# A depthwise convolution inside a tuned kernel: from diagonal products and VectorE taps to 128x32 products over shifted copies

## The chip, the cores and the metric

The kernel runs on one core of a Trainium2 chip. It is one program of 256 tokens through a stack of layers. The metric is the device time in microseconds; below, PE is TensorE (matrix products and transposes), DVE is VectorE, ACT is ScalarE, and SP is the engine whose queue issues nearly all DMAs.

## The reference, cut to what matters

The network is six feed-forward blocks with four mixers between them, each behind a norm; activations are 256 x 1024 in float32. The change is in the first mixer, which joins a convolution module and a sliding-window attention:

```python
z = h @ w_in                        # u, gate (512 each), q (512), k, v (128 each)
a = u * sigmoid(gate)               # 256 tokens x 512 channels
y = conv_general_dilated(a, w, padding=[(30, 0)],   # 31 taps, causal,
        feature_group_count=512) + b                # each channel by itself
yf = layer_norm(y) * ln_g + ln_b    # over the 512 channels
a_out = silu(yf)
b_out = sliding_window_attention(q, k, v, sinks)
return concatenate([a_out, b_out]) @ w_out
```

So output channel c at token t is a sum of 31 products of one channel's own past: `y[t, c] = sum_j w[j, c] * a[t - 30 + j, c] + b[c]`. The other parts in their order: two feed-forward blocks around this mixer and one behind it (F1, then the mixer "even", F3, F4), forgetting attention (fox), a feed-forward block (F6), an mLSTM mixer, a feed-forward block (F8), an attention with relative positions (rel), a last feed-forward block (F10) and a norm.

## The kernel before, in words

**Tiling.** The 256 tokens are two blocks b = 0 and 1 of 128 tokens. A projection is written as three products in a reduced float32 format (`mm3`): operands are split into a high and a low part (`hl` for weights, `xt` for activations), and high*high, high*low and low*high are added in PSUM. Each has 128 rows of the sum, 128 tokens as weight columns and 512 (at times 256) moving columns. Weights come from DRAM in units of 1024 columns into tiles of tag `b4`, and VectorE and ScalarE split them (`split`). Products of attention, and of the convolution, are in plain float32 and are recorded by the profiler twice each; transposes (`tr`) are products with an identity.

**Who sets the order.** The program is recorded first (`Rec`), each operation with an engine, an estimated duration, a key and the tiles it reads and writes; a line number in the trace is therefore that of a helper (`mm` L280, its matmul call at L293; `tr` L295, L298; `load` L300, L302; `store` L314, L316; `act` L199, L213; `tt` L220, L223; `stt` L237, L242). Then `schedule` (L319) simulates the engines: on each, among the operations that are ready at its time, the lowest key goes first, and a tile gets a buffer of its tag when one comes free. What results is a fixed order for each engine, written out as such. A table `NUDGE` shifts the keys of single labels by a number of weight units; `TAGS` sets columns and counts of the buffers (tag, type, columns, buffers, place), `CFG` a few leads. The two PSUM tags `acc` and `mm` have four banks of 512 columns each.

**The stage of the convolution** (`even`, L1260). Both blocks' u and gate are projected; ScalarE takes tanh of the gate, VectorE multiplies, and PE transposes the 128 x 512 result (L1298 to 1301) so that channels lie on partitions: four channel tiles of 128. ScalarE copies them behind 30 columns of zeros into two `aT` tiles, which hold 286 columns for each channel tile. Then with `cg=6` six quarters (8 taps each, 7 in the last) of the 31 taps are done on PE: channel tile 0 wholly, and the last two quarters of channel tile 1. Each tap is a product of a 128x128 diagonal matrix of its weights with the tap's 128 shifted columns, for each block by itself. The diagonals are loaded from DRAM, 8 taps in one tile. The other 75 of the multiply-adds (half of tile 1, all of tiles 2 and 3) run on VectorE over both blocks at once, 256 columns each:

```python
r.mm(bank[:, 0:P], d[:, j * P:(j + 1) * P], tap(ct, b * P + 8 * q + j, P), ...)   # PE
r.stt(ys, tap(ct, j, 2 * P), w, ys, ALU.mult, ALU.add)                            # VectorE
```

Results lie in the tile y (`yT`). For each block PE transposes y back, VectorE takes mean and variance (L1400), ScalarE normalizes, PE transposes again, and the activation follows; then the output projection (`outproj`) runs over four operand tiles, first those of the attention (2, 3), then those of the convolution (0, 1). Queries, keys, scores and softmax of the attention lie between.

**The start.** `consts` (L502) loads the input x in four pieces of 128x512, two for each block, with keys -30 + 0.15 b + 0.75 h, so the first halves of both blocks come before the second halves.

## Time and profile before

| | us |
|---|---|
| three runs | 1587.45, 1584.86, 1586.29 |
| median | 1586.29 |
| profiled execution, its own time | 1587.08 |
| its span in the trace | 1585.3 |
| PE busy | 1548.6 |
| DVE busy | 1217.4 |
| ACT busy | 938.1 |

Busy time counts an engine's instructions where at least one is running. The span goes from the first to the last instruction; the profiled execution takes 1.8 us longer than it. PEclk is the share of TensorE's full clock that was granted. A duration of one PE record is longer than the distance to the next, since products are pipelined: rates are read from blocks of many, durations from the last of a block. "Idle before" and the releaser in brackets tell what an engine waited for.

### The profile page before, as it was taken

The page shows a single profiled execution, that of the slowest core. Times are in us where ns is not written, and L with a number is a line of the kernel's source. Part 1 is how long each engine was busy: PE and PEld are TensorE (multiplying, and loading weights), DVE is VectorE, ACT ScalarE, POOL GpSimd, SP SyncE. Part 2 cuts the span into 40 slices and gives each one's busy share as a digit, 9 for nine tenths or more (in the row PEclk, how much of TensorE's full clock was granted, in tenths as well). Part 3 has the DMA queues.
Part 4 walks back from the last instruction along what each step waited for, and adds up shares of the span by engine and source line. Part 5 has one row for each costly group of instructions (what it writes and reads, how often), then busy time and mean ns, then how long its engine had stood idle before and what let it go on. Part 6 is the DMA issues. An engine that isn't in the chain of part 4 may idle for free.

```text
span 1585.3 us, 21242 instructions
## 1 busy us (share of the span) xinstructions
PE 1548.6 (98%) x7546; PEld 1266.6 (80%) x7546; DVE 1217.4 (77%) x2137; ACT 938.1 (59%) x1480; POOL 1.9 (0%) x8
## 2 busy tenths in 40 slices
PE   8999999999999999999999999999999999999998
PEld 6888878788887888787787887788877887788886
DVE  6555689798878869776899687898788674788784
ACT  6444545865555656456875565656566566765562
POOL 0000000000000000000000000000000000000000
PEclk9999999999999999999999999999999999999999
DMA  8556466447474475643664475455463755464560
GB/s 329 199 186 210 164 219 222 136 169 232 146 269 156 152 242 166 223 155 125 208 207 166 168 259 196 130 184 188 158 212 134 245 174 178 165 216 149 188 231 35
DMA packets 86779, 296.92 MB, mean 187 GB/s; under 512 B 9552, under 2 KB 13072, under 8 KB 86672
## 3 DMA queue, kind: packets, MB, share of 16 engines
q1 hardware_dynamic: 86384, 295.03, 55.1%
q8 instruction: 59, 0.97, 0.2%
q10 hardware_dynamic: 288, 0.52, 0.1%
q14 instruction: 48, 0.39, 0.1%
HBM read 294.44 MB, written 1.08 MB: 186 GB/s over the span
## 4 chain that ended last, share of the span: by engine, by line
PE 90%; DVE 6%; ACT 1%; issue 1%; DMA 1%; SPq 0%; POOLq 0%; POOL 0%; DVEq 0%; ACTq 0%
PE mm L293 59%; PE acc L293 27%; PE mm L298 4%; DVE hl L223 1%; DVE b L242 1%; DVE s L242 1%; ACT b L213 1%; DVE b L223 1%; DMA b<-in_w 1%; DVE x L242 1%; DMA x<-in_x 0%; DVE xt L223 0%; DVE s L233 0%; DVE b L254 0%; ACT L213 0%
## 5 line engine op out<-in xcount | busy, mean ns | idle before, releaser
L293 PE MATMUL mm<-hl,xt 128*128 128x512 f32 (+1 forms) x4104 | 983.6, 393 | 5.6 <-DVE xt L223 1.9
L293 PEld LDWEIGHTS mm<-hl,xt 128*128 128x128 f32 x4104 | 758.1, 188 | 168.7 <-DVE xt L223 4.8
L223 DVE TENSOR_TENSOR hl<-b,hl 128x1024 fp32r<-128x1024 f32 (+1 forms) x554 | 660.7, 1212 | 147.5 <-PE mm L293 70.5
L213 ACT ACTIVATE hl<-b 128x1024 fp32r<-128x1024 f32 (+1 forms) x554 | 572.5, 1052 | 325.4 <-PE mm L293 196.3
L293 PE MATMUL acc<-hl,gt 128*128 128x512 f32 x1584 | 385.7, 393 | 1.2 <-DVE gt L223 0.7
L293 PEld LDWEIGHTS acc<-hl,gt 128*128 128x128 f32 x1584 | 296.8, 189 | 63.9 <-DVE gt L223 1.9
L213 ACT ACTIVATE b<-mm,s 128x256 f32<-128x256 f32 (+2 forms) x150 | 77.3, 520 | 157.6 <-PE mm L293 151.1
L223 DVE TENSOR_TENSOR b<-b,b 128x1024 f32<-128x1024 f32 (+2 forms) x112 | 116.8, 1057 | 10.9 <-DMA b<-in_w 10.1
L298 PE MATMUL mm<-cst,b 128*128 128x128 f32 (+1 forms) x648 | 96.2, 276 | 9.7 <-DVE b L223 4.3
L298 PEld LDWEIGHTS mm<-cst,b 128*128 128x128 f32 (+1 forms) x648 | 77.5, 141 | 32.7 <-DVE b L223 7.0
L242 DVE SCALAR_TENSOR_TENSOR b<-mm,s,b 128x256 f32<-128x256 f32 x102 | 48.9, 479 | 63.2 <-ACT b L213 62.9
L293 PE MATMUL acc<-hl,xt 128*128 128x512 f32 x384 | 93.2, 395 | 0.9 <-DVE hl L223 0.9
L213 ACT ACTIVATE b<-b,s 128x256 f32<-128x256 f32 (+2 forms) x184 | 77.8, 450 | 24.9 <-DVE b L223 14.9
L293 PEld LDWEIGHTS acc<-hl,xt 128*128 128x128 f32 x384 | 70.6, 188 | 17.3 <-DVE hl L223 1.3
L223 DVE TENSOR_TENSOR gt<-mm,gt 128x512 fp32r<-128x512 f32 (+1 forms) x72 | 46.1, 642 | 32.7 <-ACT gt L213 32.4
L213 ACT ACTIVATE gt<-mm 128x512 fp32r<-128x512 f32 (+1 forms) x72 | 39.7, 553 | 41.7 <-PE mm L298 37.8
L213 ACT ACTIVATE b<-mm 128x512 f32<-128x512 f32 (+3 forms) x84 | 45.2, 546 | 13.8 <-PE mm L298 10.7
L242 DVE SCALAR_TENSOR_TENSOR s<-s 128x1 f32<-128x1 f32 (+2 forms) x248 | 45.4, 183 | 7.4
L213 ACT ACTIVATE b<-x 128x512 f32<-128x512 f32 x44 | 27.5, 627 | 25.8 <-DVE x L223 12.4
L242 DVE SCALAR_TENSOR_TENSOR hl<-b,cst,hl 128x512 fp32r<-128x512 f32 x48 | 33.1, 745 | 7.7 <-issue 7.6
L213 ACT ACTIVATE hl<-b,cst 128x512 fp32r<-128x512 f32 x48 | 32.7, 719 | 4.1 <-PE mm L293 3.3
L213 ACT ACTIVATE xt<-mm 128x512 fp32r<-128x512 f32 x40 | 23.4, 593 | 15.8 <-PE mm L298 14.9
(79 smaller groups left out, 597.9 us busy)
## 6 DMA issues: line engine op xcount, KB each, us to landing
b<-in_w SPq DMA_DIRECT2D x512, 512.0 KB, 5.1
g<-in_gains SPq DMA_DIRECT2D x16, 512.0 KB, 6.8
b<-in_diag SPq DMA_DIRECT2D x8, 512.0 KB, 4.6
b<-dr SPq DMA_DIRECT2D x16, 256.0 KB, 5.7
g<-in_relb SPq DMA_DIRECT2D x4, 512.0 KB, 4.7
b<-in_diag SPq DMA_DIRECT2D x4, 448.0 KB, 7.9
x<-in_x SPq DMA_DIRECT2D x4, 256.0 KB, 2.8
b<-in_w SPq DMA_DIRECT2D x4, 256.0 KB, 6.0
```

What stands on the lines that cost most here:

```text
L213: return self.nc.scalar.activation(self.res(out), self.res(in_), func, **kw)
L223: lambda: self.nc.vector.tensor_tensor(self.res(out), self.res(a), self.res(b), op), key=key)
L242: lambda: self.nc.vector.scalar_tensor_tensor(self.res(out), self.res(a), self.res(s), self.res(b), op0, op1, **kw), key=key)
L293: lambda: self.nc.tensor.matmul(self.res(out), self.res(l), self.res(r), start=start, stop=stop, **(dict(skip_group_check=True) if again e ...
L298: lambda: self.nc.tensor.transpose(self.res(out), self.res(in_), self.res(ident)), key=key)
```

## The change

The convolution goes wholly to PE, and VectorE does none of it.

- The transposed a goes into one tile `aT` of tag `b4`, 128 partitions x 4 channel tiles x 288 columns (30 of zeros, 256 tokens, 2 of zeros), with one ScalarE copy for each block. SP stores it to a new DRAM tile `da` of 512 rows (channels) x 288 columns, in two pieces: 158 columns for block 0, 130 for block 1.
- For each channel tile SP loads the weights (`cw`, 128 x 1024) and, for q = 0 to 3, the rows of `da` shifted by q columns: 32 partitions x 4 groups x 284 columns. Partition 32 q + c of the tile `taps` then holds channel c of each group g of 32 channels, shifted by q.
- A product with 128 rows (4 shifts x 32 channels) and 32 weight columns therefore sums four taps of 32 channels: 8 steps m of 4 taps make the 31 (the 32nd has weight zero), and four groups g write to the four quarters of the partitions of one PSUM bank. 32 products of 256 moving columns (both blocks) make a channel tile, 128 in all; one ScalarE instruction for each channel tile adds the bias.
- The loads of x have keys -30 + xb b + 0.2 h with xb = 1: block 0's two halves come first. Their planned price is by the same rate as that of other loads.
- `b4` tiles have 1152 columns instead of 1024, `aT` 516 instead of 572; `b2` has 10 buffers instead of 11, `s` 14 instead of 16. Tiles of `b4` that were 1024 wide say so now.
- The table of nudges is another one, of some 900 entries.

```diff
-            rows = 16 if psum == 2 else P
+            rows = {"dr": 16, "da": 512}.get(tag, P)
...
+        elif ls[1] == 32:
+            d = 115.0
...
-        o = self.op("DMA", max(nbytes / (360.0 if key > 0 else 250.0), 453.0), [src], [out],
+        o = self.op("DMA", max(nbytes / 360.0 + 0, 453.0), [src], [out],
...
-                r.load(x[:, h * 512:(h + 1) * 512], ..., P * 2048, key=-30 + 0.15 * b + 0.75 * h)
+                r.load(x[:, h * 512:(h + 1) * 512], ..., P * 2048, key=-30 + self.c["xb"] * b + 0.2 * h)
...
-        T2 = 30 + 2 * P
-        a2 = [r.t("aT", 2 * T2, name="aT") for _ in range(2)]
+        T2 = 32 + 2 * P
+        aT = r.t("b4", 4 * T2, name="aT")
+        av = aT[:, :].rearrange("p (c t) -> p c t", c=4)
+        da = r.t("da", name="da")
+        dv = da[:, :].rearrange("(c p) t -> p c t", c=4)
...
-                for ct in (2 * i, 2 * i + 1):
-                    r.copy(tap(ct, 30 + b * P, P), pt[:, ct * P:(ct + 1) * P])
...
-                    for j in range(n):
-                        r.mm(bank[:, 0:P], d[:, j * P:(j + 1) * P], tap(ct, b * P + 8 * q + j, P), ...)
...
-                    r.stt(ys, tap(ct, j, 2 * P), w, ys, ALU.mult, ALU.add)
...
+            r.copy(av[:, :, 30 + b * P:30 + b * P + P], pt[:, :].rearrange("p (c t) -> p c t", c=4), key=key)
+            t0 = 0 if b == 0 else 30 + P
+            r.store(dv[:, :, t0:30 + P + b * (P + 2)], av[:, :, t0:30 + P + b * (P + 2)], ..., key=key)
...
+            kp = self.pos(1, u0 + 3) - self.c["vp"] + 2 * ct
+            w, B = r.t("b4", 1024, name="cw"), r.t("b4", 4 * 284, name="taps")
+            r.load(w[:, :], self.a["cw"][ct], P * 4096, key=kp - 2, after=self.near(kp - 2))
+            B3 = B[:, :].rearrange("p (g t) -> p g t", g=4)
+            for q in range(4):
+                r.load(B3[32 * q:32 * q + 32], da[P * ct:P * ct + P, q:q + 284].rearrange("(g c) t -> c g t", g=4), 128 * 284 * 4, key=kp)
...
+            for m in range(8):
+                for g in range(4):
+                    o = g * 284 + 4 * m
+                    r.mm(bank[32 * g:32 * g + 32, 0:256], w[:, (4 * m + g) * 32:(4 * m + g + 1) * 32], B[:, o:o + 256], m == 0, m == 7)
+            r.end(kp)
+            r.act(y[:, 256 * ct:256 * ct + 256], bank[:, 0:256], AF.Identity, bias=cbi[:, ct:ct + 1], key=kp)
...
-    g=(F32, 1024, 3, 0), aT=(F32, 572, 4, 0), b4=(F32, 1024, 9, 0), b2=(F32, 512, 11, 0), b1=(F32, 256, 6, 0), s=(F32, 32, 16, 0),
+    g=(F32, 1024, 3, 0), aT=(F32, 516, 4, 0), b4=(F32, 1152, 9, 0), b2=(F32, 512, 10, 0), b1=(F32, 256, 6, 0), s=(F32, 32, 14, 0),
...
-    "F1 D0 b0 p": -1.5, "F1 D0 b1 p": 5, "F1 D1 b0 p": -5.5, "F1 D1 b1 p": -1.75, "F1 D10 b0 p": -6.5, "F1 D10 b1": 2.25,
```

**What moves on PE in the convolution.** Before, on PE, the 92 products of diagonals stand in twelve groups of 7 or 8 between scores (`mm<-b,b 128x256`), transposes (`mm<-cst,b`) and products of the attention's values (`acc<-b,b`); `aT` is the shifted input, `b` beside it a tile of diagonals:

```order
L298 MATMUL mm_191<-cst_68,b_156 128x128
L293 MATMUL mm_188<-aT_120,b_134 128x128 x8
L293 MATMUL mm_191<-b_155,b_139 128x256
...
L293 MATMUL mm_188<-aT_120,b_133 128x128 x8
L293 MATMUL mm_188<-aT_120,b_131 128x128 x8
L298 MATMUL mm_189<-cst_68,b_146 128x128 x4
L298 MATMUL mm_191<-cst_68,b_149 128x128 x4
L293 MATMUL acc_181<-b_147,b_154 64x128 x4
L293 MATMUL mm_189<-aT_120,b_132 128x128 x8
```

After, the 128 products stand in blocks of 32, one for each channel tile, here the first two, with one transpose of a key between them (this listing gives the output's shape, 32x256, where the profile gives that of the weights):

```order
L295 MATMUL mm_190<-hl_81,xt_105 128x256
L295 MATMUL mm_191<-b_132,b_137 32x256 x32
L300 MATMUL mm_189<-cst_71,b_155 128x128
L295 MATMUL mm_188<-b_133,b_134 32x256 x32
L300 MATMUL mm_190<-cst_71,b_143 128x128 x4
L300 MATMUL mm_189<-cst_71,b_150 128x128 x4
L295 MATMUL mm_191<-b_159,b_142 128x256
```

The third and the fourth block of 32 stand behind each other a little later, directly ahead of the transposes of the layer norm.

**What moves on SP there.** Before, loads of diagonals stand among the weight loads, none of which reads a result of the program:

```order
L302 DMA b_131<-in_diag 128x1024
L302 DMA b_132<-in_w 128x1024
L302 DMA b_133<-in_w 128x1024
L302 DMA b_134<-in_diag 128x1024
L302 DMA g_116<-in_gains 128x1024
L302 DMA b_135<-in_w 128x1024
```

After, the second store (130 columns) and the shifted loads stand there; `in_cw` are the weights of the taps, `in_swab` biases of the attention:

```order
L318 DMA da_62<-b_130 128x4x130
L304 DMA b_138<-in_w 128x1024
L304 DMA b_131<-in_w 128x1024
L304 DMA g_118<-in_swab 128x1024
L304 DMA b_132<-da_62 32x4x284
L304 DMA b_133<-da_62 32x4x284
L304 DMA b_130<-in_w 128x1024
L304 DMA b_132<-da_62 32x4x284
```

The fourth load into `b_132`, the taps of channel tile 0, stands nine rows behind the first; loads of channel tile 1 into `b_133` and of weights lie between.

**What moves on PE at the entry to the fourth feed-forward block (F6).** Before, the transposes of the norm of block 0 stand ahead of 36 products of the output projection of the forgetting attention (`acc<-hl,xt`):

```order
L293 MATMUL acc_184<-hl_79,xt_95 128x512
L298 MATMUL mm_191<-cst_68,b_139 128x128 x4
L298 MATMUL mm_190<-cst_68,b_144 128x128 x4
L293 MATMUL acc_181<-hl_77,xt_102 128x512
L293 MATMUL acc_181<-hl_78,xt_102 128x512
```

After, they stand behind these, directly ahead of products that read their result (`mm<-hl,xt`, the gate projection of F6):

```order
L295 MATMUL acc_183<-hl_85,xt_98 128x512
L300 MATMUL mm_188<-cst_71,b_147 128x128 x4
L300 MATMUL mm_190<-cst_71,b_151 128x128 x4
L295 MATMUL mm_189<-hl_87,xt_105 128x512
L295 MATMUL mm_189<-hl_88,xt_105 128x512
```

On the way from the second into the third feed-forward block (F3 to F4), PE has before: two transposes, 36 products `acc<-hl,gt`, 8 transposes of the norm, 30 products `mm<-hl,xt`; after: two transposes, 12 products `acc<-hl,gt`, 8 transposes, 30 products. From the mLSTM mixer on, PE's order is the same in both, row for row.

## Rows read from the trace of the kernel before

**Rows 1.** The page: busy time, and the chain that ended last by engine.
```profile
PE 1548.6 (98%) x7546; PEld 1266.6 (80%) x7546; DVE 1217.4 (77%) x2137; ACT 938.1 (59%) x1480; POOL 1.9 (0%) x8
...
PE 90%; DVE 6%; ACT 1%; issue 1%; DMA 1%; SPq 0%; POOLq 0%; POOL 0%; DVEq 0%; ACTq 0%
```

**Rows 2.** Windows: stretch, length, busy PE, PEld, DVE, ACT, POOL; clock, DMA, GB/s.
```profile
240.00:280.00 40.00, 38.88 (x324) 35.06 (x325) 36.49 (x124) 24.05 (x69) 0.00 (x0) 1.00 0.65 222
280.00:320.00 40.00, 37.35 (x188) 29.99 (x186) 33.55 (x84) 32.70 (x62) 0.00 (x0) 1.00 0.42 134
```

**Rows 3.** Old convolution on PE: group (ns min/median/max); one block in PE's timeline.
```profile
L293 PE MATMUL mm<-aT,b x184: 270/275/377, 244.1 to 276.2; 128*128 128x128 f32 x184
...
256.32 3.84 PE L293 MATMUL mm<-aT,b 128*128 128x128 f32 x32
```

**Rows 4.** PE's timeline around half-width tiles; windows of `acc` at one block's start.
```profile
246.07 1.13 PE L293 MATMUL mm<-b,b 64*128 64x256 f32 x8
247.14 3.84 PE L293 MATMUL mm<-aT,b 128*128 128x128 f32 x32
...
255.74 0.66 PE L293 MATMUL acc<-b,b 128*64 128x128 f32 x8
...
265.69 1.09 PE L293 MATMUL acc<-b,b 128*64 128x128 f32 x16
...
255.73:255.75 0.02, 0.01 (x2) 1.00 0.00 0
```

**Rows 5.** Groups of DVE's instructions: the taps (count, busy us, mean ns).
```profile
L242 DVE SCALAR_TENSOR_TENSOR b<-aT,cst,b 128x256 f32<-128x256 f32 x75 | 31.1, 475 | 0.0
```

**Rows 6.** DMA issues (count, KB, us to landing); issue durations of the small tile's loads.
```profile
b<-dr SPq DMA_DIRECT2D x16, 256.0 KB, 5.7
...
b<-in_diag SPq DMA_DIRECT2D x4, 448.0 KB, 7.9
...
out<-b SPq DMA_DIRECT2D x2, 256.0 KB, 2.5
...
L302 SPq DMA_DIRECT2D b<-dr x16: 326/382/551, 695.7 to 1031.7; - x16
```

**Rows 7.** The chain in order of time: twelve products of 512 columns.
```profile
38.35 2.72 PE acc L293 x12
```

**Rows 8.** Timelines of DVE and ACT at the layer norm; PE's waits, 200 to 300 us.
```profile
273.97 0.69 DVE L1400 BATCH_NORM_STATS2 s<-mm 128x6 f32<-128x512 f32 x1
...
277.19 0.77 ACT L213 ACTIVATE b<-mm,s,s 128x512 f32<-128x512 f32 x1
...
PE acc L293 <- ACT b L213: 2.9, 3, 1.4
```

**Rows 9.** PE's timelines at 485 and 667 us, wait in brackets; windows there.
```profile
485.74 1.26 PE L298 MATMUL mm<-cst,b 128*128 128x128 f32 x8 [0.80 <-DVE b L223]
487.27 0.74 PE L293 MATMUL mm<-hl,xt 128*128 128x512 f32 x2 [0.27 <-ACT xt L213]
489.21 6.65 PE L293 MATMUL mm<-hl,xt 128*128 128x512 f32 x28 [1.21 <-DVE xt L223]
...
667.03 1.52 PE L293 MATMUL mm<-hl,xt 128*128 128x512 f32 x6
670.77 0.44 PE L298 MATMUL mm<-cst,b 128*128 128x128 f32 x2 [2.22 <-DVE b L242]
672.69 1.97 PE L298 MATMUL mm<-cst,b 128*128 128x128 f32 x8 [1.49 <-DVE b L223]
674.31 4.74 PE L293 MATMUL acc<-hl,gt 128*128 128x512 f32 x12
...
671.30:678.10 6.80, 5.41 (x17) 4.64 (x18) 4.89 (x17) 3.43 (x9) 0.00 (x0) 0.50 0.24 80
```

**Rows 10.** PE's timeline at the start: the first products.
```profile
9.69 4.30 PE L293 MATMUL mm<-hl,xt 128*128 128x512 f32 x12
```

**Rows 11.** What SP's queue waited for: us in total, times, longest.
```profile
SPq L302 <- DVE hl L223: 966.8, 406, 14.1
```

## The prediction

> **What bounds the kernel now.** I read the page first. TensorE (PE) is busy for 1548.6 of 1585.3 us, and the chain that ended last runs through PE for 90% of the span [rows 1]. So a change is worth what it takes off PE's queue, plus or minus what PE waits. Next the stage of the convolution, from the windows by 40 us: PE idles 1.1 us between 240 and 280 us and 2.7 us between 280 and 320 us, while VectorE is busy for 36.5 of the 40 us of the first [rows 2]. Taking 75 taps off VectorE is therefore no gain by itself: VectorE is nearly full there, but PE hardly waits for it. What has to be priced is PE's own convolution, then each place where the new order makes PE wait.

> The profiled execution took 1587.08 us, 1.8 us beyond its span; the median of the three runs is 1586.29. I work out a difference against the span and put it on the median.

> **The change, part by part.**

> *The old convolution on PE.* All 184 records of `mm<-aT,b` go: 92 products of 128x128, two records each [rows 3]. The block of 32 from 256.32 on spans 3.84 us, the last 0.275 of it one record's own duration, so one record follows another after (3.84 - 0.275)/31 = 0.115 us, and all of them cost 21.2 us.

> *The new one.* 128 products, again two records each (no fp32 product in this trace has fewer), so 256 records with 32 weight columns and 256 moving columns. The trace has no such form; its neighbours bound it. Products with 64 weight columns (`acc<-b,b`): a block of 8 records spans 0.66 us, one of 16 spans 1.09 us [rows 4]. Eight more cost 0.43 us, 0.054 each, half of a full-width record; about 0.2 us of a block is fixed. So two column halves overlap wholly. With 256 moving columns and two row halves, 8 records take 247.14 - 246.07 = 1.07 us; less the fixed 0.2 that is 0.109 each, so one stream alone would cost 0.218. With four column quarters at once a record costs 0.218/4 = 0.0545 and the convolution 256 x 0.0545 = 14.0 us; with two at once 27.9; with one at a time 55.8. PE's order after has the new products in three uninterrupted runs, so 3 x 0.2 = 0.6 us for entering and leaving. I take four at once, 14.6 us, because the halves overlap without loss, and because both of the first two records of such a block are already running in the 0.02 us after it begins [rows 4], that is, PE does not hold a second product back behind the first one's other record. One at a time is out, since the halves overlap. PE: -21.2 + 14.6 = **-6.6 us** (ends: -6.6 and +7.3).

> [...]

> *VectorE.* 75 multiply-adds (31.1 us busy) [rows 5], three first taps and two additions of partial sums go. VectorE is freed of some 32 us, but PE's waits there are short [rows 2], so I credit it only inside the stage's sum below.

> *DMA traffic.* The 12 loads of diagonals, 5.9 MB, go; four loads of weights (2.1 MB), two stores (0.6 MB) and 16 loads of shifted rows (2.3 MB) come. The queues are not the bound, so less traffic counts zero. What counts is the round trip, on which the first convolution waits: copy out of PSUM, store, store landed, four loads landed. Copy with its signals 0.8 us; issue 0.4; landing 2.5 us, as the 256 KB store at the end; then in SP's order the fourth load of the first channel tile stands nine DMAs behind its first, 9 x 0.38 = 3.4 us of issue; landing between the 2.5 us of that store and the 5.7 us of the loads from the small DRAM tile [rows 6]. Sum: 9.6 to 12.8 us. On PE there stand, between the second block's transposes and the first 32-column product, 36 products of 512 columns, 2.72/12 = 0.227 us each [rows 7], 48 of 256 columns at half of that, 8 score products (16 records, 1.3 us) and 9 transposes (0.1 us each): 15.8 us. The cover is longer, so I count **zero**; the upper end is the rival below. SP waits there for the store, and behind it stand the weight loads of the output projection, used 20 us later.

> *The layer norm behind the convolution.* Before, its second transposes had 3 us of products ahead of them. Afterwards only 8 transposes, 16 small products and 4 transposes (2.4 us) stand between the first and second transposes of block 0, while the chain between them, from the statistics at 273.97 to the end of ScalarE's 0.77 us at 277.96 with a signal on each side, takes 4.4 us [rows 8]. New wait: 2.0 us. The next norm's transposes are followed at once by products of their own result: 1.5 us, the 0.27 and 1.21 us that the kernel before waits where it does this [rows 9]. Of the 2.9 us that PE waits for ScalarE's softmax in this stage [rows 8] I leave 0.5. Together 4.0 us after, against the 1.1 and 2.7 us of idle time before [rows 2]: about **0** (ends -2 and +2).

> *The order elsewhere.* A new table moves the work up to the mLSTM stage; from there on PE's order is the same row for row, so nothing is gained or lost after about 960 us. Three places count. Between the second and third feed-forward blocks PE now waits 2.9 us. Of the 36 products that covered the norm's chain 12 remain (2.7 us); with the last gate's transposes (0.4) and a new wait for its copy (1.5) that makes 4.6 us against a chain of 5.7 us (from 667.03 to 672.69, where the kernel has little else in between [rows 9]), so 1.1 more, and the 1.5 us behind the norm's transposes stay: 4.1 us, **+1.2**. Into the fourth feed-forward block, the transposes of block 0 stood ahead of 36 products of another operand and now stand ahead of products of their own result (1.3 us as above), and those of block 1 come 0.9 us early for their chain: **+2.2**. At the start the input of block 0 comes first, so the first products no longer stand behind transposes of a late load; they start near 8.7 us instead of 9.69 [rows 10], but wait again for the other block: **-0.7** (ends -1.7 and +1). One buffer of 512 columns fewer, two short ones fewer and a wider pool: the waits of the trace are not for those buffers; zero, +-1.

> Sum: -6.6 + 0 + 0 + 1.2 + 2.2 - 0.7 = -3.9. Of the three places I price from waits alone, fillers that I don't see shorten some; I take -4.5, so **1581.8 us**.

> **The rivals.**

> *A, two at a time.* If PE starts products strictly in order and a product's two records stand together, only neighbours overlap, a record costs 0.109 and the convolution 28.5 us: +7.3 instead of -6.6, so 1581.8 + 13.9 = **1595.7**, slower than before. It decides as soon as a record costs more than about 0.08 us. For it: no row has more than two tiles. Against it: the two records that begin together [rows 4]. [...] Chance 0.09.

> *B, the round trip is late.* The store or the loads stand behind weight loads on SP that wait for VectorE's splits: SP waits for such a split 406 times, 2.4 us each [rows 11]. With two of these ahead the chain is 12.8 + 4.8 = 17.6 us, and with landings of 7.9 instead of 5.7 us [rows 6] 19.8, against a cover of 15.8: PE waits 4 us at the first convolution and the gain is gone: **1586**. For it: SP's order puts two weight loads between the second store and the first shifted load. Against: their splits are done by then, VectorE being freed. Chance 0.18.

> *C, the clock stays up.* [...] Chance 0.13.

> *D, not quite four.* Four products side by side read four streams of moving columns at once, the halves only two, and no row tells how far that goes. If only three run at a time, a record costs 0.218/3 = 0.073 and the convolution 19.2 us: -2.0 instead of -6.6, so 1581.8 + 4.6 = **1586.4**. For it: no row has more than two streams. Against it: two streams cost no more than one. [...] Chance 0.12.

> **How the numbers follow.** Forecast 0.50, between 1578.5 and 1585; A 0.08; B 0.17; C 0.13; D 0.12. 0.2% is 3.2 us, about what a measurement can tell here, so faster means below 1583.1. Faster: 0.40 of the forecast's 0.50, C, and 0.02 of B: 0.55. Same: 0.10 of the forecast, 0.11 of B and 0.11 of D: 0.32. Slower (above 1589.5): A, 0.04 of B and 0.01 of D: 0.13. The range must leave out no more than 0.2: from 1576 (C with the low ends of the start and the stage) to 1589 (B with its high end), which leaves out A and the tails.

> **What the profile after would show.** PE's `mm<-b,b` with 32 weight columns: 256 records, in three runs of 14 to 15 us in all (four at once), 19 (D) or 28 (A). PE waiting at the first of them for a DMA (B) or not at all. About 2 us before the norm's second transposes. A granted clock of 1.00 throughout (C). Stages from mLSTM on as long as before. If PE's busy time falls by 6 us and the span does not, the new waits are larger than I priced; if the busy time falls by less than 3, the price of a record is wrong.

## The result and the profile after

The changed kernel takes **1601.19 us** (median of four runs, 1596.24 to 1603.09) where the kernel before takes 1586.05: a ratio of 1.009, 95% interval 1.0066 to 1.0115. Run again on another chip it took 1602.28 against 1587.70, 1.0093 (1.0076 to 1.011). It is slower by some 15 us; 1581.8 was forecast, with 1589 as the upper end.

The profile is of its shortest run, 1596.24 us, so 9.2 of the 15 us can be read from it. The page gives PE a little more busy time than before, not 6 us less, and more of the chain outside PE [rows 1]:

```profile
PE 1549.5 (97%) x7618; PEld 1256.7 (79%) x7618; DVE 1188.7 (75%) x2055; ACT 941.2 (59%) x1474; POOL 1.9 (0%) x8
...
PE 87%; DVE 8%; DMA 2%; issue 2%; ACT 2%; SPq 0%; POOLq 0%; DVEq 0%; POOL 0%; ACTq 0%
```

To see where, I count PE's products of 512 columns, 6024 in every kernel here, and take the time from the start of one to the start of another (the first row: from the start of the span), in us. The last two columns are experiments told below.

| products | stage | before | after | old conv., new table | all_rows | f6_all_rows |
|---|---|---|---|---|---|---|
| to 300 | start | 81.3 | 80.6 | 86.2 | 80.6 | 81.5 |
| 300 to 750 | F1 | 105.4 | 105.4 | 105.3 | 105.3 | 105.3 |
| 750 to 1050 | convolution, attention | 120.5 | 121.3 | 141.7 | 117.1 | 118.1 |
| 1050 to 1650 | F3 | 142.3 | 140.3 | 159.4 | 141.0 | 140.5 |
| 1650 to 1950 | F3 to F4 | 76.8 | 78.7 | 80.3 | 78.8 | 80.4 |
| 1950 to 2550 | F4 | 140.7 | 140.7 | 140.4 | 140.4 | 140.4 |
| 2550 to 2850 | into fox | 94.9 | 95.0 | 93.7 | 93.7 | 93.3 |
| 2850 to 3600 | fox output, **F6** | **193.1** | **203.4** | **206.0** | **205.8** | **191.8** |
| 3600 to 6023 | the rest | 622.8 | 621.6 | 623.3 | 622.2 | 623.3 |

Two places carry the loss: the convolution's stage gains nothing, and F6, 500 us behind it, loses 10 us.

**The convolution.** PE's timeline of the changed kernel, the rows of the 32-column products (start, us, group, wait ahead of it):

```profile
245.94 5.35 PE L295 MATMUL mm<-b,b 128*32 128x256 f32 x64 [3.56 <-ACT b L213]
...
251.48 3.66 PE L295 MATMUL mm<-b,b 128*32 128x256 f32 x64
...
264.99 7.11 PE L295 MATMUL mm<-b,b 128*32 128x256 f32 x128
```

At full clock 128 records span 7.11 us, 0.0555 each; the four tiles together would take 14.4 us where 14.0 and 0.6 were forecast. But PE stands for 3.56 us ahead of the first, and the first block takes 5.35 instead of 3.66. The releaser in brackets is ScalarE, whose instruction ended last; the trace's record of landings shows the other one: the fourth load of the tile landed at 245.75, and PE's sequencer stood from 240.54 to 245.78 in its wait for that landing. The windows of the stretches with half the clock (stretch, length, busy PE, PEld, DVE, ACT, POOL, clock, DMA, GB/s) show one right there, and three more; before there was one, of 6.8 us [rows 9] (the last microseconds of both programs, also at half the clock, are left out):

```profile
247.30:250.70 3.40, 3.40 (x40) 2.16 (x36) 0.00 (x0) 1.35 (x5) 0.00 (x0) 0.50 1.05 314
298.50:305.30 6.80, 6.15 (x15) 4.36 (x16) 6.32 (x20) 3.99 (x8) 0.00 (x0) 0.50 0.08 25
670.50:677.30 6.80, 6.33 (x19) 4.99 (x20) 5.70 (x14) 3.65 (x10) 0.00 (x0) 0.50 0.45 148
851.40:854.80 3.40, 3.11 (x10) 1.94 (x8) 0.57 (x1) 1.54 (x2) 0.00 (x0) 0.50 0.00 0
```

So 20.4 us run at 0.50 of the clock instead of 6.8. The first block shows what that costs: 3.40 of its 5.35 us lie there, and it takes 1.69 us more than the 3.66 of the second. PE is busy for 19.0 us of the 20.4, against 5.4 before; as an estimate half of such time is lost, some 6.8 us more than before, which is why the busy time did not fall.

**F6.** PE's timeline of the changed kernel there:

```profile
841.63 7.11 PE L295 MATMUL mm<-hl,xt 128*128 128x512 f32 x30 [0.91 <-DVE hl L223]
850.96 2.15 PE L295 MATMUL mm<-hl,xt 128*128 128x512 f32 x5 [2.23 <-DVE hl L223]
```

All that PE waited for from 800 to 890 us (us in total, times, longest):

```profile
PE mm L295 <- DVE hl L223: 4.2, 4, 2.2
PE mm L295 <- DVE xt L223: 2.3, 1, 2.3
PE mm L295 <- DVE b L223: 1.4, 1, 1.4
PE mm L295 <- ACT hl L213: 0.3, 1, 0.3
```

PE waits for split weights (`hl`), which it does not do for more than 0.95 us at a time in the kernel before. VectorE's timeline shows a split that first waits 4.27 us until PE frees a buffer, after which several are due at once:

```profile
837.77 1.23 DVE L223 TENSOR_TENSOR hl<-b,hl 128x1024 fp32r<-128x1024 f32 x1 [4.27 <-PE mm L295]
```

That alone does not explain the loss, since the kernel before has a wait of the same length there and loses nothing:

```profile
834.90 2.36 DVE L223 TENSOR_TENSOR hl<-b,hl 128x1024 fp32r<-128x1024 f32 x2 [4.27 <-PE mm L293]
```

SP's waits from 820 to 870 us differ more: it can't load on for up to 19 us, because the raw tiles wait for their splits (first line: after, second: before), and from 800 to 870 us it issues 17 loads of weights where the kernel before issues 25:

```profile
SPq L304 <- DVE hl L223: 49.0, 13, 19.0
...
SPq L302 <- DVE hl L223: 34.9, 14, 13.8
```

### The profile page after: what moved, and what is told of

Its sections match the earlier page's. It is cut to its first block, busy times and chain, and to the rows that moved or that the text cites. A ratio compares the mean times of both kernels' runs of the same rounds, so it can differ in the third digit from the quotient of the medians.

```text
span 1594.4 us, 21313 instructions
## 1 busy us (share of the span) xinstructions
PE 1549.5 (97%) x7618; PEld 1256.7 (79%) x7618; DVE 1188.7 (75%) x2055; ACT 941.2 (59%) x1474; POOL 1.9 (0%) x8
## 4 chain that ended last, share of the span: by engine, by line
PE 87%; DVE 8%; DMA 2%; issue 2%; ACT 2%; SPq 0%; POOLq 0%; DVEq 0%; POOL 0%; ACTq 0%
PE mm L295 57%; PE acc L295 26%; PE mm L300 4%; DVE hl L223 3%; DVE s L242 1%; DVE b L223 1%; DMA b<-in_w 1%; DVE b L242 1%; ACT b L213 1%; DVE x L242 1%; DVE xt L223 0%; DMA b<-dr 0%; ACT hl L213 0%; DVE s L233 0%; DMA x<-in_x 0%
## 5 line engine op out<-in xcount | busy, mean ns | idle before, releaser
L223 DVE TENSOR_TENSOR b<-b,b 128x1024 f32<-128x1024 f32 (+1 forms) x110 | 116.3, 1073 | 6.1 <-DMA b<-in_w 5.1
L223 DVE TENSOR_TENSOR gt<-mm,gt 128x512 fp32r<-128x512 f32 (+1 forms) x72 | 46.0, 642 | 27.8 <-ACT gt L213 27.3
L213 ACT ACTIVATE b<-mm 128x512 f32<-128x512 f32 (+3 forms) x84 | 45.6, 554 | 14.5 <-PE mm L300 8.8
L295 PE MATMUL mm<-b,b 128*32 128x256 f32 (+2 forms) x464 | 38.6, 378 | 3.6 <-ACT b L213 3.6
L295 PEld LDWEIGHTS mm<-b,b 128*32 128x32 f32 (+1 forms) x464 | 24.7, 149 | 17.8 <-ACT b L213 5.3
```

Source lines behind the costliest of these rows:

```text
L213: return self.nc.scalar.activation(self.res(out), self.res(in_), func, **kw)
L223: lambda: self.nc.vector.tensor_tensor(self.res(out), self.res(a), self.res(b), op), key=key)
L295: lambda: self.nc.tensor.matmul(self.res(out), self.res(l), self.res(r), start=start, stop=stop, **(dict(skip_group_check=True) if again e ...
```

## The experiments

### Whose loss is it: the convolution's or the table's

Two kernels cross the two: the convolution of before with the new table, and the new one with the old table; a third puts back only a part of the table.

```diff
 # old_conv_new_table: the kernel before, with
-NUDGE = {...}     # before
+NUDGE = {...}     # the changed kernel's
 # new_conv_old_table: the changed kernel, with the table of before (entries "even conv..." kept)
 # fox_table_back: the changed kernel, with the entries "fox ..." and "unit110" upward of before
```

> The convolution, buffers and start of the kernel before, with only the new table of nudges; from the second feed-forward block (F3) on, PE's order is that of the changed kernel row for row. Theory 'table': the 10 us that the changed kernel loses between 814 and 965 us come from the new order there, whatever convolution stands ahead; then this kernel loses 6 to 11 us there too and takes 1592 to 1598 us. Rival 'convolution': the loss comes from what the new convolution brings (more DMAs, another wait, one buffer fewer) and only shows up later; then this one is within 3 us of the kernel before there, 1583 to 1589 us.

Measured: 1642.83 us, 1.0331 (1.0311 to 1.0351) of before. The sum is far outside both expectations: under a table that was not made for it the old convolution loses 21 us in its own stage and 17 in F3. But F6 answers the question. PE's order there is that of the changed kernel, and so, nearly one for one, are PE's waits from 845 to 940 us, 500 us behind a wholly different convolution:

```profile
PE mm L293 <- DVE hl L223: 4.4, 4, 2.4
PE mm L293 <- DVE xt L223: 2.3, 1, 2.3
PE mm L293 <- DVE b L223: 1.4, 1, 1.4
PE mm L293 <- ACT hl L213: 0.3, 1, 0.3
```

F6 takes 206.0 us here, 203.4 after and 193.1 before. The new order loses there without the new convolution.

> The changed kernel with the table of the kernel before, except the entries of the convolution itself. Theory 'table': no loss in the fourth feed-forward block (F6); what is left is the convolution's stage, -7 us of PE work against a wait of 3 to 5 us at the first new product and the half clock behind it, so 1582 to 1589 us. Rival 'convolution': the loss of 6 to 10 us in F6 is there again, 1592 to 1600 us. The old table was not made for these durations, so other waits may come, up to 5 us.

Measured: 1677.01 us, 1.0545 (1.0528 to 1.0561). Neither theory expected that. It loses 35 us in the convolution's stage and 49 in F6, in an order that neither of the two kernels has. All that it shows is that the old table, given to durations and buffers that it was not made for, makes an order that loses more than either.

> The changed kernel with the old table entries of the forgetting attention and of the weight units behind it alone; up to there PE's order is that of the changed kernel, and from the 3072nd product of 512 columns on (in F6) that of the kernel before. Theory 'table': the stages up to 760 us as in the changed kernel, the loss of 10 us in F6 down to 0 to 3 us, the time 8 to 10 us below the changed kernel. Rival 'convolution': the loss stays at 6 us or more.

Measured: 1613.85 us, 1.0152 (1.0128 to 1.0176): not 8 to 10 us below the changed kernel but some 9 above it (23.9 us above the kernel before, where the changed one is 15). The sum is a miss, and yet F6 gives the other half of the cross. From the 3072nd product on, PE's order is by form that of the kernel before, as expected. From there to the 3600th product it takes 125.7 us; the kernel before takes 125.8, the changed one 134.6, and the old convolution with the new table 136.0. PE's waits there, from 859 to 985 us, are those of the kernel before within 0.1 us:

```profile
PE mm L295 <- DVE hl L223: 0.9, 1, 0.9
PE mm L300 <- DVE b L242: 0.7, 1, 0.7
```

So in F6 the old order loses nothing behind the new convolution, and the new order loses behind the old one: the loss there belongs to the order. What this kernel loses lies ahead of F6, where the two tables meet in the forgetting attention: from the 2850th to the 3072nd product it takes 93.6 us, where the kernel before takes 67.3 and the changed one 68.8. Up to there it ran the changed kernel's order, and PE waited 8.13 us at the first new product, far more than the 3.56 us above, so this wait varies.

### F6 with another order

Entries of F6 and of the weight units from 126 on were searched anew, by the planner's own plan, the rest being left as it is.

```diff
 # f6_replan: 111 entries of NUDGE "F6 ..." and "unit126" to "unit160" changed, for instance
-    "unit127": 2, "unit129": 2.75, "unit131": -0.5, "unit134": 2.75, "F6 G0 b0": 7.5, "F6 D8 b1 p": 7.25,
...
+    "unit127": 2.75, "unit129": 1.25, "unit131": -0.25, "unit134": -2, "F6 G0 b0": -1, "F6 D8 b1 p": 8.25,
...
```

> The changed kernel with 111 other entries of the table, only of the fourth feed-forward block (F6) and of the weight units from 126 on; PE's order is that of the changed kernel up to the 2874th product of 512 columns (some 770 us) and from the 3660th on. Theory 'early splits': in the changed kernel F6 loses 9 to 10 us because weight pieces were split 20 to 44 us ahead of their use and hold 10 to 12 of the 16 buffers of split weights, so that the rest are split just in time; with another order there the loss falls to 0 to 3 us and the time by 7 to 11 us. Rival 'convolution': the loss comes from what the convolution does to the queues and buffers, and no order there takes it away; it stays at 6 us or more.

Measured: 1587.80 us against 1587.70 of before: 1.0 (0.9987 to 1.0013), 14.5 us below the changed kernel on the same chip, more than the 7 to 11 that I expected. From the 2850th to the 3600th product it takes 191.7 us, where the changed kernel's profile from that chip has 205.6. The waits of PE from 800 to 890 us are one:

```profile
PE mm L295 <- DVE xt L223: 1.4, 1, 1.4
```

Where each split piece of weights lay and when it was first used can be read by laying the order of each engine beside the trace. Of the 16 buffers, pieces that were split over 20 us ahead of their use hold 8.4 on average from 835 to 870 us in the changed kernel, 3.2 in this one. But in the kernel before it is 8.5, with no such loss. What sets the changed kernel apart is the stretch ahead: from 815 to 835 us it splits 12 pieces where both others split 18, and 8 of the pieces split from 835 to 870 are used within 0.5 us of being ready, against 2 before and none here. So "early splits hold the buffers" does not explain the loss by itself, and the count hangs on the bound: pieces split over 15 us ahead hold 10.5 buffers in the changed kernel, 9.7 in this one and 10.1 before. What the counts leave is that nothing was in reserve; that this is the cause is argued, since no run changes it alone.

### The wait at the first new product

> The changed kernel as it is, beside the three others on the same chip. Theory: the wait at the first new product varies from one execution to the next (3.56 us in the profile of the changed kernel, 8.1 us at the same place in the kernel with the old entries of the forgetting attention, which has the same order up to there), and that is the 5 us by which its runs differ (1596.2 to 1603.1). A profile that takes 1600 us or more should show a wait of 7 us or more there; one of 1596 us, 3 to 4 us.

Measured: 1602.28 us, 1.0093; the profiled run took 1604.42.

```profile
249.88 6.40 PE L295 MATMUL mm<-b,b 128*32 128x256 f32 x64 [4.99 <-ACT b L213]
```

The wait there is 4.99 us, not 7 or more, so the theory is wrong: it explains 1.4 of the 8 us between the two profiles. The rest is spread: 27.3 us at half the clock instead of 20.5 (behind waits that both profiles have, but at 208, 488 and 805 us in this one alone, at 298 us in the first alone), and some half microseconds elsewhere.

In the changed kernel's trace, the landings of SP's DMAs around the first shifted loads read so (issue, what, landing; all in us; `b<-da` are the shifted loads of 142 KB):

```
226.34 da<-b      230.39        233.54 b<-da      242.28
226.81 b<-in_w    232.24        235.71 b<-in_swab 243.04
227.36 b<-in_w    233.49        236.89 b<-in_w    245.32
227.81 g<-in_swab 235.65        237.73 b<-da      245.75   (fourth load of tile 0)
230.46 b<-da      236.82
230.89 b<-da      237.72
231.62 b<-in_w    239.63
232.11 b<-da      240.40
232.58 b<-da      241.05
233.05 b<-da      241.72
```

Two things: the DMAs from 233.54 on are issued within 0.1 us of the landing of the eighth before them (233.49 and 233.54, 235.65 and 235.71, 236.82 and 236.89, 237.72 and 237.73). The trace's semaphore records show the same over the whole run: SP's DMAs report their landing on eight semaphores in turn (588 of the 590 that have an eighth before them use its semaphore), and not one of the 588 is issued before that eighth has landed. And the landings come one behind another, those of 512 KB 1.2 to 2.3 us behind the one before, the shifted loads mostly 0.56 to 0.9 (the first 1.17, the fourth of tile 0 0.43). SP's waits from 226 to 246 us, which before had 0.4 us for landings in the same stretch, show it too; the last line is the store, which the first shifted load needs in any case:

```profile
SPq L304 <- DMA b<-in_w: 3.5, 2, 1.9
SPq L304 <- DMA b<-da: 1.7, 4, 0.6
SPq L304 <- DMA g<-in_swab: 1.7, 1, 1.7
SPq L304 <- DMA da<-b: 1.5, 1, 1.5
```

Is it the count of loads, or their form? Three kernels keep PE's order and change the loads alone.

```diff
 # one_load: the first of four loads writes 128 partitions x 1136 columns, the three others left out
+s = bass.AP(s.tensor, s.offset, [[n, P], [0, 4], [1, 284]])          # n: row length of da
 # by_group: four loads, each 128 partitions (32q + c) x 284 columns of one group g
+s = bass.AP(s.tensor, s.offset + 32 * g * n, [[1, 4], [n, 32], [1, 284]])
 # all_rows: the same with partition 4c + q, and the weights' rows likewise
+s = bass.AP(s.tensor, s.offset + 32 * g * n, [[n, 32], [1, 4], [1, 284]])
```

> The changed kernel with one load for each channel tile in the place of the first of its four, with the same number of bytes (128 rows, each written four times), and the other three left out; what it loads is not the shifted rows. PE's order is the same. Theory 'lanes': the fourth shifted load is issued 7 us behind the first because each DMA of the queue waits until the eighth before it has landed, so with 12 DMAs fewer the wait of 3.56 us at the first new product falls below 1 us, and the half clock behind it does not come: 3 to 5 us less up to 307 us. Rival 'bandwidth': the transfers are late because the 16 DMA engines are full there whatever the count; the wait stays at 2 us or more.

Measured: 1596.17 us against 1589.94, 1.0034 (1.0016 to 1.0052). PE does not wait at the first new product, no half clock follows, and the stage is 5.8 us shorter (115.6):

```profile
242.80 3.66 PE L295 MATMUL mm<-b,b 128*32 128x256 f32 x64
```

SP waits for no landing but that of the store (1.5 us). That fits "lanes"; but the one load also fills 128 partitions where the four fill 32 each, so it does not decide. "Bandwidth" as I put it falls, since the wait is gone; yet the 16 DMA engines are busy throughout in both kernels, and what differs is how much they move (DMA share and GB/s at the end; first the changed kernel, then this one):

```profile
226.00:246.00 20.00, 16.44 (x112) 14.08 (x114) 8.92 (x28) 13.04 (x29) 0.00 (x0) 1.00 1.02 258
...
226.00:246.00 20.00, 20.00 (x171) 16.36 (x173) 8.97 (x29) 12.84 (x27) 0.00 (x0) 1.00 1.00 342
```

> The changed kernel with the same 16 loads of the same bytes at the same places of the queue, but each fills 128 partitions with 284 columns (one group of 32 channels, all four shifts) instead of 32 partitions with four times 284. Theory 'lanes' (each DMA of the queue waits until the eighth before it has landed, and the count makes the delay): the wait at the first new product stays, 3 to 8 us, and the time is that of the changed kernel within 2 us. Rival 'partitions' (a load into 32 partitions only is slow to land): the landing of these loads falls from 7.4 us to 5 or less, the wait at the first new product below 1 us, and the time is 4 to 8 us below the changed kernel, as it was with one load for each tile.

Measured: 1606.18 us, 1.0126 (1.0107 to 1.0146), slower than the changed kernel. PE waits twice:

```profile
246.48 0.62 PE L295 MATMUL mm<-b,b 128*32 128x256 f32 x2 [3.04 <-DMA b<-da]
252.37 4.93 PE L295 MATMUL mm<-b,b 128*32 128x256 f32 x58 [5.28 <-DMA b<-da]
```

"Partitions" seems to fall, but the landing records show that the experiment changed something else: each of these loads has 5 completion records, where those of the changed kernel have 16, and they land 1.2 to 2 us apart. Two things differ from the changed kernel at once, the partitions that a load fills and its outermost dimension (the four shifts here, the 32 channels there). So this run is inconclusive on its question.

> The changed kernel with the shifted copies laid out otherwise: partition 4c + q instead of 32q + c (the weights' rows likewise), so that each of the 16 loads fills all 128 partitions with 284 columns, as with by_group, but with the 32 channels as the outermost dimension of the transfer instead of the four shifts. Same loads, bytes and places. by_group could not tell 'lanes' from 'partitions', because its transfers were slower in themselves (1.2 to 2 us from one landing to the next, where the changed kernel's small loads take 0.7). Theory 'partitions': the small loads now land 0.4 us behind one another (at the rate of the weight loads) instead of 0.7; seven stand ahead of the fourth, so the wait at the first new product falls by some 2 us, to 1 to 3 us. Rival 'count alone': 0.7 us each as before, the wait stays at 3.5 to 5.7 us and the time at that of the changed kernel, 1596 to 1604 us.

Measured: 1594.93 us against 1588.12, 1.0044 (1.0029 to 1.006): 6.8 us above the kernel before, where the changed kernel is 15.1 and 14.6 above it. The small loads now land 0.37 to 0.42 us behind one another where nothing else lies between (238.85, 239.27, 239.68, 240.05), the fourth of tile 0 at 243.05. PE starts without a wait, because each load now brings one group of channels with all its shifts, and the first product needs only the first load; the wait for the fourth stands inside the first block, which takes 0.7 us more than 3.66:

```profile
242.39 4.34 PE L295 MATMUL mm<-b,b 128*32 128x256 f32 x64
...
246.93 3.66 PE L295 MATMUL mm<-b,b 128*32 128x256 f32 x64
```

The form decides, somewhat more than I expected: PE loses 0.7 us where it lost 3.56. The fourth load lands 2.7 us earlier, 0.6 of it because it is issued earlier (237.14 instead of 237.73), the rest because it and those ahead of it take less time. What fewer places in the queue would do by themselves, no run tells. A load of 142 KB landed some 0.7 us behind the one before it into 32 partitions (changed kernel) and 0.4 us into 128 (this one); what sets these times is not shown. "Count alone" is out.

### Why the 32-column products run side by side

```diff
-            for m in range(8):
-                for g in range(4):
+            for g in range(4):
+                for m in range(8):
```

> The changed kernel with the 32 products of a channel tile in another order: eight on one quarter of the columns, then eight on the next, instead of the four quarters in turn. Theory 'neighbours': products run side by side because neighbours in the queue lie on different quarters; 16 records on one quarter then run one by one, 0.218 us each, a block of 32 products takes some 14 us instead of 3.6, the convolution 56 us, and the kernel is 35 to 42 us slower than the changed one. Rival 'PE looks ahead': it takes products of other quarters past those that wait, and the block stays below 6 us.

Measured: 1633.83 us, 1.029 (1.0275 to 1.0306), 31.5 us above the changed kernel.

```profile
263.26 11.50 PE L295 MATMUL mm<-b,b 128*32 128x256 f32 x64
...
284.60 21.98 PE L295 MATMUL mm<-b,b 128*32 128x256 f32 x128
```

"Neighbours" holds in the main: 0.172 us a record (21.98/128) instead of 0.0555. This 0.172 is a mean. On one quarter one record starts 0.216 us behind the other in the trace (263.503, 263.718, 263.934), so one stream costs what I took, 0.218, and four in turn run at a quarter of it. But at each change of the quarter eight records start in pairs, 6 or 30 ns apart (265.877 and 265.883, 266.093 and 266.123): the first four of the next quarter run beside the last four, two products, of the one before, and its first product begins before the last one that stands ahead of it. So PE does look ahead, but here by no more than that; it saves some 0.8 us at each change, and this makes the kernel 31.5 us slower instead of 35 to 42. In the order of the change, a window of 0.04 us behind the first product's start has four records begun; as records of one quarter start 0.216 us apart, these lie on four quarters, and PE does not wait for a product's second record before it begins the next product:

```profile
245.93:245.97 0.04, 0.03 (x4) 1.00 0.58 131
```

### Versions made from this

Two tables were made for the whole front half, with a planner that counts eight DMAs under way and 6.5 us for a shifted load to land.

```diff
+            if e == "DMA":
+                if len(lanes) >= 8:
+                    t = max(t, lanes[-8])
             o.start = t
             o.end = t + d
+            if e == "DMA":
+                lanes.append(o.end + max(o.lat, 6500.0))
```

> The same convolution and buffers as the changed kernel, the same instructions; the table is another one up to F6, made with two things that the planner did not count: at most eight loads of SP's queue under way, and 6.5 us from issue to landing for the shifted rows, whose four loads of a tile need not wait for each other. The four loads of channel tile 0 stand together, three rows behind the second store, instead of spread over ten. Theory: the loss was the order and the wait, not the 32-column products; the fourth load is issued within 3 us of the first, the wait at the first new product falls from 3.6 to 5.7 us to below 2, F6 loses no more than 2 us, and the time is 1580 to 1585 us, below the kernel before by 2 to 6 us. Rival: what is gained at one place comes back at another (the products' gain of 7 us is eaten by half-clock stretches behind other waits); then 1586 to 1592 us.

> As replan_a, with another table: the four loads of channel tile 0 stand directly behind the second store, ahead of all weight loads, and the second block of 32 new products stands behind scores and transposes instead of directly behind the first. Theory: the fourth load is issued within 2 us of the first and landed before PE is there, no wait at the first new product above 1 us; 1578 to 1584 us. Rival: 1586 to 1592 us, as above.

Measured: 1587.18 us, 0.999 (0.9978 to 1.0002), and 1587.14, 0.9989 (0.9981 to 0.9998), against 1588.54. The rival was right. In both kernels PE does not wait at the first new product, and F6 takes 195.7 us in replan_a and 191.6 in replan_b. Here is where the gain went: in replan_b all four tiles take 3.66 us, without a wait, but PE then waits at the entry to F3, at 295.81, 298.60 and 313.81 (its timeline):

```profile
295.81 1.26 PE L300 MATMUL mm<-cst,b 128*128 128x128 f32 x8 [1.89 <-DVE b L223]
298.60 12.88 PE L295 MATMUL mm<-hl,xt 128*128 128x512 f32 x42 [1.54 <-ACT xt L213]
...
313.81 6.41 PE L295 MATMUL mm<-hl,xt 128*128 128x512 f32 x27 [1.46 <-DVE xt L223]
```

and the clock halves behind the first of these (its window):

```profile
297.90:304.70 6.80, 6.10 (x14) 4.33 (x15) 6.06 (x22) 4.00 (x9) 0.00 (x0) 0.50 0.37 126
```

From the 750th to the 1650th product replan_b takes 263.9 us, the kernel before 262.8: what the convolution gives, the entry to F3 takes (in replan_a, 265.1 us).

The last version takes the two findings together: the order of f6_replan and the layout of all_rows.

> f6_replan with the layout of all_rows. f6_replan has no loss left in F6 and took the time of the kernel before; what it still has is the wait of 3.73 us at the first new product and 1.7 us of half clock behind it. If that wait shrinks by 2 us or more, the time is 2 to 5 us below that of f6_replan, 1582 to 1586 us, and below the kernel before; with 'count alone' it stays at 1586 to 1589 us.

Measured: **1582.67 us** against 1588.12 of before on the same chip, 0.9965 (0.9952 to 0.9977). It beats both kernels. The first new product starts without a wait, and F6, in the table above, has no loss:

```profile
244.80 3.66 PE L295 MATMUL mm<-b,b 128*32 128x256 f32 x64
248.65 3.66 PE L295 MATMUL mm<-b,b 128*32 128x256 f32 x64
```

Two things stay open. Half-clock stretches remain, 17.0 us of them against 6.8 before (at 208, 297 and 481 us). And F6 was searched anew here and not in the kernel before, so how much of the gain is the convolution's no run tells; in the table its stage gives 2.4 us and F6 1.3.

## Why the prediction was wrong, point by point

- **The new products' price** (14.6 us): right. 14.4 us at full clock; rivals A and D fall. The steps behind it held: one stream at 0.218 (0.216 measured), four at 0.0545 (0.0555).
- **The round trip, counted at zero**: the first step that failed. I put issue at 3.4 us and landing between 2.5 and 5.7, in all 9.6 to 12.8 us with the copy. From the second store (226.34) to the fourth load's landing (245.75) it took 19.4 without it. The store took 4.1 us instead of 2.9. Issue of the loads took 7.3, since SP waits for the eighth DMA before to land, which I had not looked for; landing took 8.0, since small loads into 32 partitions cost 0.7 us each in the queue. Rival B had the size (19.8, a wait of 4) by another mechanism: the waits of rows 11, for splits, were not it. The cover was even longer than forecast, 17.0 us (225.43 to 242.38) instead of 15.8. PE waited 3.56 us here, 4.99, 5.68 and 8.13 in others with the same order up to there.
- **The order elsewhere**, "the three places count": the step that failed by most. The two entries that I priced came out nearly right: F3 to F4 +1.9 (forecast +1.2; the 2.9 us of before are the three waits of rows 9, 2.28, and two of 0.19 and 0.47 behind them), and into F6 0.81 + 2.29 = 3.1 us of waits where I had 2.2 more than next to nothing. But I read PE's order only where transposes stand, and took it that products of the feed-forward blocks run without waits, as they do before. In F6 the order of the splits had moved too, and the loss behind the entry was 7 us, gone with the old order there (125.7 against 134.6).
- **The clock**: rival C asked whether a stretch at half the clock would go; it stayed (6.8 us at 670), and three came. The low end of the range, 1576, rests on what C would bring; no run shows that term by itself. What there is: in f6_all_rows, whose half-clock stretches lie at 208, 297 and 481 us, the stage into fox takes 93.3 us, where the changed kernel takes 95.0. I had priced new waits by their length alone. Waits of 1.5 to 3.6 us, at 246, 297 and 851, were followed by 3.4 or 6.8 us at half the clock, which cost 1.6 to 3.1 us more; the one of 2.29 us at 802 was not.
- **The layer norm** (0): right as a sum, not in its parts: 0.44 us at the second transposes instead of 2.0, and 2.5 behind the next norm (1.53, 0.79, 0.20) instead of 1.5; the half clock behind those was not priced. **The start** (-0.7): not shown. This profile has 80.6 against 81.3, but the second one of the same kernel has 81.4. **F3** gained 1.9 us that I had not seen; by which part of the order, no run tells.
- **The sum**: in this profile +0.8 in the convolution's stage instead of 0 and -6.6, and +10.3 in F6 instead of +2.2. In that stage PE's work fell by 6.8 (21.2 to 14.4), and the wait of 3.56 and half the clock behind it (1.7) and at 298 us (3.1) ate it up. The remaining 5 us between it and the median are waits and half-clock stretches that vary from run to run; they are not settled in detail.
- "If the busy time falls by 6 us and the span does not" was meant to tell waits from price. It did not: busy time at half the clock hid the gain.
- Two slips change nothing: the loads of diagonals are 6.0 MB, not 5.9, and A and B stand at 0.09 and 0.18 in their own lines but at 0.08 and 0.17 in the sum.

With the two faults mended, the change brings 5.4 us. That it lies near the 4.5 of the first sum is luck: by the table the stages give -2.4 (convolution), -1.8 (F3), +3.6 (F3 to F4), -1.6 (into fox) and -1.3 (F6), not the -6.6, +1.2, +2.2 and -0.7 of the sum.

## What to carry to other kernels

Where a change re-plans the order of a saturated kernel, compare the order on every engine over the whole stretch that moved, the splits and loads too, not only at the waits that you know; a plan made for one set of durations can lose more, far from the edit, than the edit gains. A chain over DRAM is priced by what stands in the queue: how many transfers are under way, and how long each holds the one behind it, which here went with the partitions that a transfer fills (142 KB: 0.7 us into 32, 0.4 us into 128). A wait on PE is priced with the clock behind it: in the changed kernel three waits of 1.5 to 3.6 us were followed by 3.4 or 6.8 us at 0.50 of it, one of 2.29 us was not.
